# One table of issue times for the end of layer 0's first attention pass, and a longer distance between sums and their products

## The chip, the cores and the metric

The kernel runs on one core of a Trainium2 chip. The metric is the device time of one execution in microseconds (us); the kernel before has a median of 3018.23 us over three runs. PE is TensorE, PEld its weight loads, DVE VectorE, ACT ScalarE, POOL GpSimd, and SP issues the DMAs. L880 is line 880 of the kernel before.

## The reference, cut to what matters

Two layers of a transformer over 1024 image tokens in a 16 x 64 grid and 256 context tokens, width 1024, 16 heads of 64. Layer 0 mixes with neighbourhood attention (a window of 8 x 16 around each query, plus all context tokens), layer 1 with grouped attention over all tokens. Each mixer and each gated feed-forward (hidden width 2816) stands behind a root-mean-square norm with shift, scale and gate that come from a conditioning vector. All is float32 to close accuracy.

```python
def rms_norm(x, g):
    y = xf * lax.rsqrt(jnp.mean(xf * xf, axis=-1, keepdims=True) + EPS)
...
a_l = ada_norm(h, norm_mix[i], sh1_l, sc1_l)
y_l, y_c = neighbourhood_attention_mixer(a_l, a_c, ...)      # layer 0
h = h + g1_l * y_l
h = h + g2_l * swiglu_ffn(ada_norm(h, norm_ffn[i], sh2_l, sc2_l), ffn_w_in[i], ffn_w_out[i])
# the same for the context hc in layer 0
```

## The kernel before, in words

Everything is held transposed: 128 channels on the partitions, tokens along the free axis, in blocks b = 0 and 1 (512 image tokens each) and b = 2 (the 256 context tokens). For accuracy a float32 operand is split into a high and a low part, and a product is three matmuls: high by high, high by low, low by high (`dense_steps`, L770 to L772). The cast to the high part is an ACT instruction, the difference for the low part one of DVE or POOL (L682 and L684 for weights, L812 and L814 for queries and keys, L1868 and L1870 for attention outputs).

Order on each engine is fixed when the program is built. `Lanes` (the object `bg`) keeps a model clock `bg.now` in nanoseconds and a list of background jobs. A job is a Python generator: `pump(credit)` lets the first job issue PE work, where one unit of credit is three matmuls of 512 columns, and `slot(engine)` lets the first waiting piece of side work in lanes 0, 1, 2 issue one instruction on ACT, DVE or POOL. `tick` gives out several slots and one unit, `turn` a third of a unit every 227 ns.

Layer 0's attention is a sequence of *pairs*: two 128-token query tiles of one head. The first pass has three pairs a head, query tiles 0 and 1, tiles 2 and 3, and the two of the context (48 pairs; the context's have only the 256 context keys, and `pump` gets 0.7 more in them). The second pass has two pairs a head (32). A pair's stages are scores (S, X), minima (m, mX, mn), exponentials (e, L849), sums and reciprocals (sr), scaling on POOL (sc, L860), transposes on PE (T, L867), cast and difference (c, s, L875 and L880), products with the values (PV, L497), copy of the output (oc, L889), sum of its parts on POOL (r) and output through a DMA (z). A table, `ORDERA` or `ORDERB`, gives each stage its time relative to the pair's start, with a period from pair to pair (7622 and 5560 ns). `Plan` lays the pairs out by table and sorts all stages by time. In the tables stand filling entries too: PF pumps a given rate of projection work, AF, DF and GF offer a slot of ACT, DVE or POOL. `ORDERA` has three PF, four AF, five DF and three GF a pair, `ORDERB` three PF, two AF, two DF and two GF. The last phase gives its filling for three pairs more.

What fills the pairs: projections of later heads in the order (p, 0), values, (p, 1), then the output projection ("out"), with its weights' splits; DVE products that give the modulation from the conditioning vector (`ada_chunks`, L492, in lane 2, the last); and splits of finished attention outputs (`out_split0`, lane 1). Where a head's projections are not finished when they must be loaded, `until` ticks until they are.

After the plan, what is left of "out" is issued, and layer 0's feed-forward starts with the output projection of block 1 (`project`), which needs the last pair's output. Beside it run three norms: block 0, context, block 1. `norm` squares on ACT (L157), adds the squares up in two running sums (`nacc`, `nacb`) on DVE or POOL (L144), and then `ms_sum` multiplies both with a matrix of ones on PE (L190), which gives the mean to all partitions. Logarithm and exponential on ACT (L177, L179) make the reciprocal root in a tile `nrs`, and `apply` scales the block (L1173; L1305 for the context), shifts it (L1183) and splits it (L955, L952). The three norms share the tiles of the sums and `nrs`. The feed-forward's first products (`mm1`, L1461 to L1463) use a scheme with sums and differences of the blocks: P1 and P2 of five hidden tiles on block 0, with the context beside them, come first, and then P7, which needs differences of both blocks (`sums`) and of the weights.

`ms_sum` waits in the model clock before it issues its products:

```python
while len(added) < count or max(added) + 1200 > bg.now:
    yield ""
```

where `added` holds the model's times at which the running sums are done.

Of the kernel before, what the change touches and what calls it, by code (L numbers as in the profile page):

```python
# [20 lines left out]
KC = D // P  # L21
# [10 lines left out]

V_NMIX, V_NFFN, V_NFIN, V_B, V_QG, V_KG, V_C = 0, 16, 32, 40, 136, 137, 138
V_N = 154
CFG = dict(lag=3, tv=8.0, tm=5.0, t1=43.0, t2=58.0, p0=28, lo="GD", n=39, ra=2.3, rc=0.7, rq=1.1, rb=1.05, gap=263, r1=1.262, lh=300, tk='ADAG', tb=1000000000.0, tg=1, lp='GD')
PERIOD1 = 8172
ORDER1 = {
# [8 lines left out]
PERIODA = 7622  # L46
ORDERA = {
# [6 lines left out]
}  # L54
PERIODB = 5560
ORDERB = {
# [6 lines left out]
}  # L63
# [9 lines left out]
def _build(tc, nc, I, O, top):  # L73
# [62 lines left out]
    def norm(tag, src, there, n, tmp, bank, done, direct=0, line=0):  # L136


        acc, gives, added = [], [], []

        def add(sq, give, engines):
            yield engines
            i = int(bg.engine == "G")
            (v, g)[i].tensor_tensor(acc[i], acc[i], sq, ALU.add)  # L144
            bg.both((690, 1290)[i] * n / 512)
            spent = max(600 + 700 * i, bg.cost)
            added.append(bg.now + spent)
            yield from bg.sleep(spent)
            give()

        ms = None
        for kc in range(KC):
            while not there(kc):
                yield ""
            sq, give = yield from tmp.take("nsq" if kc > 1 else ("nacc", "nacb")[kc], n)
            yield "A0"
            s.activation(sq, src(kc), AF.Square)  # L157
            if kc < 2:
                acc.append(sq)
                gives.append(give)  # L160
            elif kc < KC - direct:
                bg.enter(tag, add(sq, give, "D" if direct or kc >= KC - 2 else "GD"), 800, line)
            else:
                yield from bg.sleep(700)
                if ms is None:
                    ms, free = yield from ms_sum(acc, added, KC - direct - 2, n, bank)
                yield "M"
                t.matmul(ms, lhsT=ones[:], rhs=sq, start=False, stop=kc == KC - 1)
                give()
        if ms is None:  # L170
            ms, free = yield from ms_sum(acc, added, KC - 2, n, bank, True)
        for give in gives:
            give()
        rs, give = yield from tmp.take("nrs", n)
        yield from bg.sleep(2000 if not direct else 1000)
        yield "L"
        s.activation(rs, ms, AF.Ln, bias=eps[:])  # L177
        free()
        s.activation(rs, rs, AF.Exp, scale=-0.5)  # L179
        yield from bg.sleep(1100)  # L180
        yield from done(rs)
        give()

    def ms_sum(acc, added, count, n, bank, stop=False):
        while len(added) < count or max(added) + 1200 > bg.now:
            yield ""
        ms, free = yield from bank()
        yield "M"
        for i in range(2):
            t.matmul(ms[:, :n], lhsT=ones[:], rhs=acc[i], start=i == 0, stop=stop and i == 1)  # L190
        return ms[:, :n], free
# [75 lines left out]
    def startup():  # L267

        ET = mybir.EngineType
        with ExitStack() as ph:  # L270
# [10 lines left out]
            def start(at, gen):  # L281

                heapq.heappush(todo, (at, next(count), gen))
# [9 lines left out]
            def load_raw(k, src):  # L293
                raws[k] = wraw.tile([P, D], F32, name="wr")
                if k[0] == "v":
                    dma(out=raws[k][:].rearrange("p (u n) -> p u n", u=2), in_=src.rearrange("u p n -> p u n"))
                else:
                    dma(out=raws[k][:], in_=src)

            def loads():  # L300
# [12 lines left out]
                for i in range(2):  # L313
                    load_raw(f"v{i}", W[16:18, :, i * 512:i * 512 + 512])
                    start(now + CFG["tv"], split(f"v{i}", w0))
                    yield 1.5
# [15 lines left out]
            def split(k, pool):  # L332
                hi = pool.tile([P, D], F32R, name="wh")
                lo = pool.tile([P, D], F32R, name="wl")
                ws[k] = hi, lo
                s.copy(hi[:], raws[k][:])
                yield 1.2
                v.tensor_tensor(lo[:], raws[k][:], hi[:].bitcast(F32), ALU.subtract)  # L338
# [4 lines left out]
            def c_rows():  # L343
                for w in range(2):
                    for i in range(2):
                        ps = psm.tile([P, 512], F32, name="ps1")
                        dg = tmp.tile([P, 4, P], F32, name="nsq", bufs=2)
                        v.tensor_tensor(dg[:], ident[:].unsqueeze(1).broadcast_to([P, 4, P]),
                                        silc2[:, 4 * i:4 * i + 4, w:w + 1].broadcast_to([P, 4, P]), ALU.mult)
                        t.matmul(ps[:], lhsT=ones[:], rhs=dg[:].rearrange("p a n -> p (a n)"), start=True, stop=True)  # L350
                        yield 0.8
                        s.mul(crow[w][:, i * 512:i * 512 + 512], ps[:], float(D))
                        yield 0.3

            def stat(b):
                n = BLK[b][1]
                acc = []
                for kc in range(KC):
# [10 lines left out]
                    yield 0.55  # L369
                yield CFG["tm"] if b == 1 else 2.0  # L370
                ms = psp.tile([P, 512], F32, name="ms")
# [65 lines left out]
            def first_qk(b):  # L437
# [3 lines left out]
                for kc in range(KC):  # L441
                    while (b, kc) not in ready or b == 0 and min(kc + CFG["lag"], KC - 1) not in ready:
                        yield 0.2
# [20 lines left out]

            for at, gen in [(0.0, loads()), (5.0, c_rows()), (10.0, stat(0)), (CFG["t1"], stat(1)), (CFG["t2"], stat(2)), (28.0, projections())] + \
                    [(max(9.5, a), modulation(m)) for m, a in enumerate((7.0, 13.0, 18.7, 23.0, 26.0, 30.4, 33.3, 36.2))]:
# [32 lines left out]
    class Ring:  # L499
# [4 lines left out]
        def free(self):  # L504
            return self.k < self.n or self.k - self.n in self.back
# [5 lines left out]
        def give(self, k):  # L511
            self.back.add(k)
# [31 lines left out]
    class Lanes:  # L544
# [170 lines left out]
        def tick(self, cost=1.0):  # L715

            self.now += 650
            for e in "TML" + CFG["tk"]:
                if self.busy.get(e, 0) < self.now + CFG["tg" if e == "G" else "tb"]:
                    self.slot(e)  # L720
# [299 lines left out]
    class Ffn:  # L1020
# [97 lines left out]
        def there(self, b, at, k0=0):  # L1118
            return lambda kc: (b, (kc + k0) % KC) in at and at[b, (kc + k0) % KC] <= bg.now

        def src(self, b, k0=0):
            return lambda kc: self.h[b][(kc + k0) % KC]
# [4 lines left out]
        def bank(self):  # L1127
            ps = yield from self.banks.take()
            return ps, lambda: self.banks.give(ps, after=900.0)
# [650 lines left out]
    with ExitStack() as ph:  # L1780
# [6 lines left out]
        bg = Lanes(pb)  # L1787
# [247 lines left out]
        for i, job in enumerate(bg.main[:2]):  # L2035
# [3 lines left out]
        ffn0 = Ffn(0, I["x1"], H0d, lambda m: modB[0][:, m, 0:1], lambda m, b: modB[0][:, 24 + m, which(b):which(b) + 1])  # L2039
        pairs = [[Pair0(h, ps, i) for h in range(HEADS) for i in range(3 - ps)] for ps in range(2)]  # L2040
        n = CFG["n"]
        plan = Plan([(PERIODA, ORDERA, pairs[0][:n], CFG["ra"], 0), (PERIODA, ORDERA, pairs[0][n:], CFG["rq"], CFG["gap"]),
                     (PERIODB, ORDERB, pairs[1], CFG["rb"], 0)])
        load_head(0, 0)
        masks = pb.tile([P, 2, 3, P], F32, name="masks", bufs=1)
        dma(out=masks[:], in_=I["masks"])
# [424 lines left out]
    pairs = [Pair1(h, b) for blk in range(2) for h in range(HEADS) for b in (4 * blk, 4 * blk + 2)]  # L2471
    plan = Plan([(PERIOD1, ORDER1, pairs, CFG["r1"], 0)])
# [173 lines left out]
```

## Time and profile before

| | |
|---|---|
| median of 3 runs | 3018.23 us (3011.64 to 3019.13) |
| the profiled execution | 3023.16 us, span 3021.4 us |
| mean granted TensorE clock | 0.989 |
| PE, DVE, ACT, POOL busy | 97%, 76%, 54%, 41% of the span |
| first pass, pairs 39 to 47 | output copies from 495.8 to 555.5 us |
| second pass, 32 pairs | output copies from 563.8 to 741.4 us |
| layer 0's norms for the feed-forward | products with ones at 769.80, 783.70 and 802.00 us |
| first product P7 | 861.70 us |

The profile shows one execution; its times are counted from the first instruction. "Busy" is the union of an engine's instructions, and matmuls overlap in a pipeline, so a PE that is 97% busy can still be short of its peak. A group line names line, engine, operation, output and inputs, form and count, then busy us and mean ns of one, then the idle time of the engine just before them with what ended it. A line of the timeline begins with start and duration in us, and its bracket holds the idle time before it and what ended that.

### The profile page before, as it was taken

What the parts mean: (1) busy time and instruction counts of PE and PEld (TensorE: products, weight loads), DVE (VectorE), ACT (ScalarE), POOL (GpSimd) and SP (SyncE); (2) the same over time, 40 slices, a digit from 0 to 9 for tenths busy, and PEclk for the clock granted to TensorE, in tenths of its full rate; (3) what the DMA queues carried; (4) which work ended last, traced back from release to release, by engine and by line L of the source; (5) the groups of instructions that cost most, each with busy time, mean ns of one, the idle gap of its engine ahead of it and who ended that gap; (6) DMA issues with size and microseconds to landing.
All of it is one profiled execution on the core that took longest, in us unless ns stands there. A gap on an engine that the chain in (4) does not pass through costs nothing.

```text
span 3021.4 us, 50120 instructions
## 1 busy us (share of the span) xinstructions
PE 2920.2 (97%) x16460; PEld 2506.4 (83%) x16460; DVE 2302.6 (76%) x4659; ACT 1621.6 (54%) x3739; POOL 1247.0 (41%) x1109
## 2 busy tenths in 40 slices
PE   7999999999999999999999899999999999999998
PEld 5888997888788888888888788888888878888886
DVE  7578778876798875557777588899887887776776
ACT  4345545776742322234456489899887632333444
POOL 4246556776244441121121256666643354223112
PEclk8999999999999999999999999999999999999999
DMA  7767767887545562249655523333323333224962
GB/s 265 218 216 238 229 216 232 242 238 214 197 147 192 194 221 80 88 159 323 215 190 196 164 83 94 112 98 102 107 76 124 134 140 121 102 105 150 323 217 108
DMA packets 307170, 519.03 MB, mean 172 GB/s; under 512 B 46432, under 2 KB 112096, under 8 KB 305120
## 3 DMA queue, kind: packets, MB, share of 16 engines
q1 hardware_dynamic: 306912, 515.84, 52.4%
q8 instruction: 131, 2.15, 0.3%
q14 instruction: 127, 1.04, 0.1%
HBM read 389.61 MB, written 120.18 MB: 169 GB/s over the span
## 4 chain that ended last, share of the span: by engine, by line
PE 78%; DVE 10%; DMA 4%; ACT 3%; issue 2%; POOL 2%; SPq 1%; DVEq 0%; ACTq 0%; POOLq 0%
PE pf L1461 9%; PE pf L1462 9%; PE pf L1463 9%; PE T L867 5%; PE o L497 5%; PE pf L1710 5%; PE pf L1709 5%; PE pf L1711 5%; PE ps L770 3%; PE ps L771 3%; PE ps L772 3%; PE S L2254 2%; PE S L2255 2%; DVE pT L880 1%; PE pf L1483 1%
## 5 line engine op out<-in xcount | busy, mean ns | idle before, releaser
L860 POOL TENSOR_SCALAR Pt<-Pt,rc 128x1280 f32<-128x1280 f32 (+3 forms) x288 | 298.8, 1038 | 388.1 <-ACT pT L875 137.6
L880 DVE TENSOR_TENSOR pT<-T,pT 128x256 fp32r<-128x256 f32 (+2 forms) x672 | 341.9, 535 | 35.7 <-ACT pT L875 35.2
L875 ACT CAST pT<-T 128x256 fp32r<-128x256 f32 (+2 forms) x672 | 305.0, 478 | 113.5 <-PE T L867 109.5
L867 PE MATMUL T<-ident,Pt 128*128 128x128 f32 x1952 | 303.0, 275 | 24.3 <-POOL Pt L860 23.2
L867 PEld LDWEIGHTS T<-ident,Pt 128*128 128x128 f32 x1952 | 235.0, 140 | 80.8 <-POOL Pt L860 37.0
L497 PE MATMUL o<-pT,Vt 128*128 128x256 f32 x1952 | 295.2, 290 | 2.3 <-DVE pT L880 2.2
L770 PE MATMUL ps<-ah,wh 128*128 128x512 f32 (+1 forms) x688 | 261.8, 380 | 6.5 <-ACT ah L432 2.6
L497 PEld LDWEIGHTS o<-pT,Vt 128*128 128x128 f32 x1952 | 253.8, 189 | 9.3 <-DVE pT L880 5.7
L771 PE MATMUL ps<-al,wh 128*128 128x512 f32 (+1 forms) x688 | 251.8, 366 | 3.8 <-POOL al L132 2.6
L849 ACT ACTIVATE Pt<-S,rc 128x512 f32<-128x512 f32 (+2 forms) x384 | 247.6, 655 | 9.6 <-DVE rc L841 6.1
L772 PE MATMUL ps<-ah,wl 128*128 128x512 f32 (+1 forms) x688 | 251.2, 365 | 1.4 <-DVE wl L338 1.4
L2246 DVE TENSOR_REDUCE nm<-S 128x1 f32<-128x512 f32 x256 | 169.7, 683 | 35.4 <-PE S L2255 33.7
L952 POOL TENSOR_TENSOR c<-c,c 128x512 f32<-128x512 f32 (+1 forms) x63 | 93.9, 1492 | 246.8 <-DVE c L955 89.6
L955 DVE TENSOR_TENSOR c<-c,c 128x512 fp32r<-128x512 f32 (+1 forms) x166 | 131.9, 809 | 49.3 <-ACT c L1437 34.5
L849 ACT ACTIVATE Pt<-X,rc 128x256 f32<-128x256 f32 x256 | 125.4, 490 | 67.5 <-DVE rc L841 60.8
L1437 ACT CAST wh<-c 128x512 fp32r<-128x512 f32 x112 | 68.8, 618 | 167.2 <-PE pf L1462 62.8
L772 PEld LDWEIGHTS ps<-ah,wl 128*128 128x128 f32 x688 | 131.2, 191 | 23.5 <-DVE wl L338 2.1
L770 PEld LDWEIGHTS ps<-ah,wh 128*128 128x128 f32 x688 | 131.6, 191 | 20.1 <-ACT ah L432 2.8
L1461 PE MATMUL pf<-c,wh 128*128 128x512 f32 x376 | 146.5, 390 | 0.0
L1462 PE MATMUL pf<-c,wh 128*128 128x512 f32 x376 | 146.5, 390 | 0.0
L1463 PE MATMUL pf<-c,wl 128*128 128x512 f32 x376 | 146.3, 389 | 0.0
L895 POOL TENSOR_TENSOR r<-ob 128x256 f32<-128x256 f32 x144 | 123.7, 859 | 54.5 <-ACT ob L889 53.6
(599 smaller groups left out, 9153.4 us busy)
## 6 DMA issues: line engine op xcount, KB each, us to landing
c<-in_fout SPq DMA_DIRECT2D x119, 256.0 KB, 4.0
wr<-in_wqkv SPq DMA_DIRECT2D x53, 512.0 KB, 4.3
wr<-in_adaT SPq DMA_DIRECT2D x96, 256.0 KB, 3.1
c<-in_fin SPq DMA_DIRECT2D x68, 256.0 KB, 3.0
adaw<-in_adaT SPq DMA_DIRECT2D x64, 256.0 KB, 3.8
wr<-in_wo SPq DMA_DIRECT2D x32, 512.0 KB, 4.3
wr<-in_fin SPq DMA_DIRECT2D x58, 256.0 KB, 2.8
K<-Kd SPq DMA_DIRECT2D x64, 224.0 KB, 5.1
```

Source lines behind the costliest of these rows:

```text
L497: t.matmul(o_ap, lhsT=u.V[:, kb, :], rhs=u.pT[:, i, :], start=i == 0, stop=i == len(u.blocks) - 1)
L770: t.matmul(ps, lhsT=hi[:, c], rhs=ah[:, kc, :n], start=kc == 0, stop=False)
L771: t.matmul(ps, lhsT=hi[:, c], rhs=al[:, kc, :n], start=False, stop=False)
L772: t.matmul(ps, lhsT=lo[:, c], rhs=ah[:, kc, :n], start=False, stop=kc == KC - 1)
L849: s.activation(u.Pt[:, off:off + u.wid[c]], u.S[c], AF.Exp, bias=u.min, scale=u.sign, accum_out=u.rc[:, 3 + c:4 + c])
L860: g.tensor_scalar(Pt, Pt, u.rc[:, 2:3], 1.0, ALU.mult, ALU.mult)
L867: t.transpose(T[:, i * P:(i + 1) * P], u.Pt[:, (i0 + i) * P:(i0 + i + 1) * P], ident[:])
L875: s.copy(u.pT[:, i0:i0 + n, :P], u.T[c])
L880: v.tensor_tensor(u.pT[:, i0:i0 + n, P:], u.T[c], u.pT[:, i0:i0 + n, :P].bitcast(F32), ALU.subtract)
L1461: t.matmul(ps[:], lhsT=r32(hi[:, c]), rhs=bh, start=k == 0, stop=False)
L1462: t.matmul(ps[:], lhsT=r32(hi[:, c]), rhs=bl, start=False, stop=False)
L1463: t.matmul(ps[:], lhsT=r32(lo[:, c]), rhs=bh, start=False, stop=k == 3)
```

## The change

The plan had three phases: pairs 0 to 38 by `ORDERA` at rate 2.3, pairs 39 to 47 by `ORDERA` at rate 1.1, and the second pass by `ORDERB` at rate 1.05. It now has two: pairs 0 to 38 as before, then pairs 39 to 47 and the second pass together by `ORDERB` at rate 1.12. The gap of 263 ns stands behind pair 38 in place of pair 47.

`ms_sum` gets its distance as an argument: 3600 ns of the model clock for the three norms of layer 0's feed-forward, and 1200 as before for all others.

```diff
-... rq=1.1, rb=1.05, gap=263, ...
+... rq=1.1, rb=1.12, gap=263, ...
@@ norm
         if ms is None:
-            ms, free = yield from ms_sum(acc, added, KC - 2, n, bank, True)
+
+            ms, free = yield from ms_sum(acc, added, KC - 2, n, bank, True, 3600 if tag == "norm" or tag[:2] == ("norm", 0) else 1200)
@@
-    def ms_sum(acc, added, count, n, bank, stop=False):
-        while len(added) < count or max(added) + 1200 > bg.now:
+    def ms_sum(acc, added, count, n, bank, stop=False, margin=1200):
+        while len(added) < count or max(added) + margin > bg.now:
             yield ""
@@
-        plan = Plan([(PERIODA, ORDERA, pairs[0][:n], CFG["ra"], 0), (PERIODA, ORDERA, pairs[0][n:], CFG["rq"], CFG["gap"]),
-                     (PERIODB, ORDERB, pairs[1], CFG["rb"], 0)])
+
+        plan = Plan([(PERIODA, ORDERA, pairs[0][:n], CFG["ra"], CFG["gap"]),
+                     (PERIODB, ORDERB, pairs[0][n:] + pairs[1], CFG["rb"], 0)])
```

More of the change, by code (lines that the diff above doesn't have):

```diff
@@ L34 @@
 V_N = 154
-CFG = dict(lag=3, tv=8.0, tm=5.0, t1=43.0, t2=58.0, p0=28, lo="GD", n=39, ra=2.3, rc=0.7, rq=1.1, rb=1.05, gap=263, r1=1.262, lh=300, tk='ADAG', tb=1000000000.0, tg=1, lp='GD')
+CFG = dict(lag=3, tv=8.0, tm=5.0, t1=43.0, t2=58.0, p0=28, lo="GD", n=39, ra=2.3, rc=0.7, rq=1.1, rb=1.12, gap=263, r1=1.262, lh=300, tk='ADAG', tb=1000000000.0, tg=1, lp='GD')
 PERIOD1 = 8172
```

## The prediction

> **What bounds the kernel now.** I read the head of the page first, then the busy time by stage, then in each touched stage the waits of PE and the busiest groups of DVE. Columns of a stretch: length; busy us and count of PE, PEld, DVE, ACT, POOL; granted clock; DMA share; GB/s.
>
> ```profile
> span 3021.4 us, 50120 instructions
> PE 2920.2 (97%) x16460; PEld 2506.4 (83%) x16460; DVE 2302.6 (76%) x4659; ACT 1621.6 (54%) x3739; POOL 1247.0 (41%) x1109
> ...
> 372.50:480.90 108.40, 106.48 (x746) 98.82 (x745) 77.77 (x222) 54.39 (x159) 58.27 (x64) 1.00 0.71 221
> 480.90:548.80 67.90, 59.61 (x339) 48.53 (x338) 60.06 (x160) 42.10 (x124) 44.33 (x48) 0.97 0.72 224
> 548.80:580.00 31.20, 29.06 (x191) 25.72 (x190) 26.30 (x89) 25.35 (x78) 21.35 (x25) 1.00 0.84 239
> 580.00:741.00 161.00, 155.38 (x1085) 140.26 (x1084) 126.57 (x440) 123.68 (x377) 120.11 (x141) 1.00 0.83 239
> ```
>
> PE is the bound nearly everywhere, 97% of the span. The exception is 480.9 to 548.8 us, the last nine pairs of the first pass: PE is 88% busy there, DVE also 88%, against 96.5% and 79% in the second pass from 580. So the change works where PE has room. How long a pair takes shows in the copies of its output (count, duration, first and last start), nine for pairs 39 to 47 and 32 for the second pass:
>
> ```profile
> L889 ACT COPY ob<-o x9: 586/586/587, 495.8 to 555.5; 128x512 f32<-128x512 f32 x9
> ...
> L889 ACT COPY ob<-o x32: 586/587/602, 563.8 to 741.4; 128x512 f32<-128x512 f32 x32
> ```
>
> The nine take 563.8 - 495.8 = 68.0 us, 7.55 each; a second-pass pair takes (741.4 - 563.8)/31 = 5.73. The tables say 7.622 and 5.560, so the nine follow their table and the others run behind theirs. What PE waited for in the nine pairs, and what filled DVE and PE there (busy us, mean ns, idle before):
>
> ```profile
> PE T L867 <- POOL Pt L860: 5.4, 6, 1.1
> PE o L497 <- DVE pT L880: 2.2, 6, 0.7
> ...
> L492 DVE CUSTOM_DVE_ANT_0 adaj<-adaw,crow 128x512 f32<-128x512 f32 x16 | 17.6, 1101 | 0.2
> L1870 DVE TENSOR_TENSOR al<-o,ah 128x512 fp32r<-128x512 f32 (+1 forms) x10 | 8.2, 834 | 0.0
> L814 DVE SCALAR_TENSOR_TENSOR ql<-ps,qh 128x512 fp32r<-128x512 f32 (+1 forms) x6 | 3.9, 645 | 0.0
> L684 DVE TENSOR_TENSOR wl<-wr,wh 128x512 fp32r<-128x512 f32 x4 | 3.1, 771 | 0.0
> ...
> L770 PE MATMUL ps<-ah,wh 128*128 128x512 f32 (+1 forms) x46 | 18.5, 402 | 0.0
> ...
> L497 PE MATMUL o<-pT,Vt 128*128 128x256 f32 x69 | 13.4, 303 | 2.3 <-DVE pT L880 2.2
> ```
>
> PE waits for the pair's own chain (scaled rows, transposes, split), because too little lies between its links. Of DVE's 60.06 us, 17.6 + 8.2 + 3.9 + 3.1 = 32.8 us in 36 instructions are filling, more than half of it the modulation products of line 492.
>
> **The change part by part.** *Nine pairs by the second table.* Nothing is computed less; the chain is interleaved more tightly. If the nine ran at 5.73 they would take 51.6 us, 16.4 less: the far end. They hold more projection than a second-pass pair: 46/9 = 5.1 groups of three matmuls each, against
>
> ```profile
> L770 PE MATMUL ps<-ah,wh 128*128 128x512 f32 (+1 forms) x116 | 44.2, 381 | 0.0
> ...
> L497 PE MATMUL o<-pT,Vt 128*128 128x256 f32 x266 | 42.4, 289 | 0.0
> ```
>
> 116/28 = 4.1 (161/5.73 = 28 pairs in the stretch from 580), with wider tiles (402 ns against 381). One group more is about 0.7 us by the 0.68 below. Every third pair (the context's) has less attention: 69/9 = 7.7 products with the values a pair against 266/28 = 9.5, and 1.8 fewer of half a group member's width (0.11) give back 0.2. So 5.73 + 0.5 = 6.2 to 6.3 each, 56.5 in all: a gain of 11.5 us. The near end is that DVE holds them: with all its filling left in, its 60.06 us leave 68.0 - 60.1 = 8 us to win at most, and I put 2 as the least, a quarter of that.
>
> *Slots of DVE.* The first table has five DF slots a pair, the second two: 45 become 18. Of the 36 filling instructions about 24 still fit (18, and some six that the wait for the last projections of head 14 gives out at its ticks), so 12 move into the second pass; line 492 is last in the order of the lanes, so it is these, 12 x 1.1 = 13 us. DVE falls to 47 of 56.5 us in the nine pairs. The second pass has 31.20 - 26.30 = 4.9 us of idle DVE in its first 31 us and 34.4 in the next 161, but takes the 13 in its first eight or nine pairs, about 50 us, with some 10 us idle. Bounds 0 (idle time takes all) and 8 (all inside the first 31 us); I take 2.5, nearer the idle time. The AF slots (four to two) and GF (three to two) carry what they carry in the second pass already. The modulation is needed only after the second pass, so a later end costs nothing of itself.
>
> *Rate 1.12.* 27 slots get 0.02 and 105 (35 x 3, three pairs of filling behind the last) get 0.07 more: 7.9 units. A unit is three 512-column matmuls, and the last of them stand here behind the last output copy:
>
> ```profile
> 741.10 0.39 PE L770 MATMUL ps<-ah,wh 128*128 128x512 f32 x1
> ...
> 741.78 0.39 PE L770 MATMUL ps<-ah,wh 128*128 128x512 f32 x1
> ...
> 748.05 0.40 PE L770 MATMUL pf<-ah,wh 128*128 128x512 f32 x1
> ...
> 754.03 0.49 PE L770 MATMUL pf<-ah,wh 128*128 128x512 f32 x1 [1.03 <-ACT ah L1868]
> ...
> 753.36 0.62 ACT L1868 CAST ah<-o 128x512 fp32r<-128x512 f32 x1 [4.61 <-DMA o<-Od]
> ```
>
> A unit is 741.78 - 741.10 = 0.68 us, so 5.4 us of projection move from behind the last pair into the second pass. In the pass it costs between 0 (all inside PE's idle 3.5% and the small waits) and 5.4; I take 3. Behind the last pair it gains nothing: the block's last output goes through two DMAs and a split (741.4 to 754.03, 12.6 us), and the 6.95 us of projection from 741.10 to 748.05 only cover that. With 1.6 left of it PE waits about 1 + 5.4 us at the same place. Term 0.
>
> *The distance of the sums.* Three norms of layer 0's feed-forward put their two products of ones 2.4 us (3.5 units) later into PE's order.
>
> ```profile
> 769.80 0.67 PE L190 MATMUL pf<-c,ones 128*128 128x512 f32 x1
> ...
> 783.70 0.70 PE L190 MATMUL pf<-c,ones 128*128 128x256 f32 x2 [2.39 <-DVE c L144]
> ...
> 802.00 1.12 PE L190 MATMUL pf<-c,ones 128*128 128x512 f32 x2 [2.85 <-DVE c L144]
> ...
> 803.42 0.79 PE L1461 MATMUL pf<-ah,wh 128*128 128x512 f32 x1
> ...
> 861.70 0.50 PE L1461 MATMUL pf<-ah,wh 128*128 128x512 f32 x1 [1.52 <-ACT wh L1437]
> ```
>
> The context's wait of 2.39 goes: output projections stand ready to move ahead. The 2.85 before the third (block 1) does not: the projections are over, and the first weights of the feed-forward are split only then, so a wait for those takes its place and the products (1.42 us to 803.42) follow later. The first norm (769.80) waits for nothing, so its move is a pure delay of 2.4 us for what hangs on it:
>
> ```profile
> 772.42 0.67 ACT L177 ACTIVATE c<-pf,eps 128x512 f32<-128x512 f32 x1
> ...
> 777.12 0.62 ACT L682 CAST wh<-wr 128x512 fp32r<-128x512 f32 x1 [3.06 <-DMA wr<-in_wo]
> ...
> 797.79 0.72 ACT L1183 ACTIVATE c<-c,modB 128x512 f32<-128x512 f32 x1
> ...
> 799.07 0.47 ACT L177 ACTIVATE c<-pf,eps 128x256 f32<-128x256 f32 x1
> ...
> 810.01 0.49 DVE L134 SCALAR_TENSOR_TENSOR al<-pl,modB,ah 128x256 fp32r<-128x256 f32 x1
> ...
> 814.59 0.69 ACT L177 ACTIVATE c<-pf,eps 128x512 f32<-128x512 f32 x1
> ```
>
> The three share one tile for the root (nrs): the context's logarithm (799.07) follows the last shift of block 0 (797.79), block 1's (814.59) the end of the context's apply (810.01), and from there the sums lead to 861.70, where PE waits. So the first norm's delay reaches PE's next wait, while the 2.39 saved makes PE come earlier to it. If the new place puts the logarithm behind the cast at 777.12, which waited 3.06 us for its DMA, the delay is 5 rather than 2.4. Against it, everything on ACT and DVE that waits for PE's projections moves up by 2.4. Bounds: -3 (2.39 and a little of the 2.85 kept) and +5; I take 0, between a delay and a gain of 2.4 each. PE's 1.52 at 861.70 stays.
>
> *Sum.* -11.5 + 2.5 + 3 + 0 + 0 = -6 us. The profiled execution took 3023.16 us, 4.9 above the median 3018.23 of the runs; so 3017.2 for an execution like it, 3012 for the median.
>
> [...] In the stretches 500 to 505 and 505 to 510 the granted clock was low although PE's longest wait among the pairs is 1.1 us:
>
> ```profile
> 500.00:505.00 5.00, 3.32 (x14) 2.40 (x13) 4.34 (x11) 4.09 (x14) 4.55 (x6) 0.81 0.79 253
> 505.00:510.00 5.00, 5.00 (x29) 4.40 (x28) 4.90 (x14) 2.50 (x10) 2.71 (x4) 0.85 0.61 191
> 740.00:755.00 15.00, 13.74 (x75) 11.50 (x74) 3.41 (x8) 2.87 (x5) 6.34 (x7) 1.00 0.55 158
> ```
>
> That loss was 5 x 0.19 + 5 x 0.15 = 1.7 us. [...]
>
> **The rivals.** *All of the room is won (28%).* The nine pairs run at the second pass' 5.73 (-16.4), the 13 us of DVE and the 5.4 of PE vanish half in idle time (+2), the context's 2.39 is kept (-2): about -14, that is 3004. For it: DVE is idle 34.4 us of the second pass, and its visible PE waits are short. Against: the nine carry more projection.
>
> *The nine pairs are held by DVE, and the table matters little (12%).* The least of 2 us is won, and with 3 for the rate the time is 3019. For it: DVE is busy 4.90 of 5 us from 505. Against: the filling that makes it so loses its slots.
>
> *The norms' chain costs more than the pairs win (12%).* Block 0's logarithm falls behind the cast that waits for its DMA: 5 us, and as the two running sums are shared as well, the context's norm adds its own 2.4, block 1's another: up to 9.8 at 861.70. From a delay of 6 on the kernel is slower than before; with the full one the time is 3018 - 6 + 9.8 = 3022. For it: the shared tile shows in the order 797.79, 799.07, 810.01, 814.59. Against: PE's own place moves up.
>
> *The clock falls behind the last pair (10%).* The rate takes 5.4 us of cover from a wait of 1.03, and if the clock then falls as it did at 500, the same 1.7 us is lost: -4.3, that is 3014. For it: the two rows from 500. Against: 1.00 in the row from 740. [...]
>
> **How the numbers follow.** A measurement here tells about 0.3%, 9 us, from no change. My forecast 3012 (38%) covers 3008 to 3016 by itself; the rivals 28, 12, 12 and 10%. Faster by over 0.3% (below 3009): the first rival, and a little of the forecast: 0.31. Slower by over 0.3% (above 3027): only the far part of the chain's case and what I have not seen: 0.09. Within: 0.60. The range 3001 to 3022 reaches from -17 (the first rival's ends all taken) to the chain's case.
>
> **What would show it.** The nine output copies 6.2 to 6.3 us apart; line 492 running into the second pass, by some eight pairs; second-pass pairs at about 5.8 to 5.9; after the last copy 12 to 13 us to the split of the last block, with a PE wait of 5 to 7 us; no PE wait at the context's products of ones, a new one ahead of the first feed-forward matmul, and the wait at the difference weights (861.70 before) about as long as now. I am wrong if the nine pairs stay above 7 us, if the second pass grows by over 6 us, or if the feed-forward's first wait grows by more than 4.

## The result and the profile after

The changed kernel takes 3024.23 us in the median of 8 runs, against 3017.08 for the kernel before in 8: a ratio of 1.0023, 95% interval 1.0013 to 1.0034. That is 7 us slower, small but outside the scatter; a second comparison, below, gives 1.0020 (1.0010 to 1.0030). The forecast was 3012, with 3001 to 3022 as its range.

The two profiled executions hide this: 3024.11 us after and 3023.16 before, because the one before lies 6 us above its median (3.5 us of that are lost before pair 30, where both kernels are the same: its output copy starts at 411.4 in the trace before, at 407.8 in the one after). So I compare stages within the traces and take totals from the runs.

The head of the page after, the output copies of pairs 39 to 48 and of the second pass, and the busy time by stage (columns as before). Lines from 170 on are one higher than before, from about 2040 on two:

```profile
span 3022.1 us, 50109 instructions
PE 2917.2 (97%) x16460; PEld 2504.8 (83%) x16460; DVE 2297.4 (76%) x4663; ACT 1621.4 (54%) x3739; POOL 1244.8 (41%) x1105
...
L890 ACT COPY ob<-o x10: 586/589/597, 494.8 to 546.8; 128x512 f32<-128x512 f32 x10
...
L890 ACT COPY ob<-o x32: 586/587/599, 546.8 to 735.0; 128x512 f32<-128x512 f32 x32
...
494.80:546.80 52.00, 51.38 (x313) 44.13 (x313) 43.26 (x134) 41.97 (x122) 38.77 (x43) 1.00 0.84 254
546.80:570.00 23.20, 21.43 (x140) 18.43 (x139) 20.56 (x72) 20.12 (x61) 19.03 (x21) 1.00 0.93 256
570.00:625.00 55.00, 41.09 (x276) 34.08 (x275) 45.78 (x162) 41.44 (x130) 43.12 (x48) 1.00 0.86 240
625.00:735.00 110.00, 105.53 (x731) 96.09 (x730) 83.75 (x287) 78.44 (x238) 77.62 (x89) 0.98 0.77 227
```

The nine pairs won more than forecast: 546.8 - 494.8 = 52.0 us against 68.0, and PE is busy 99% there. Not all of the 16 us is kept, because the copies of pairs 30 to 39 come 2.5 us further apart than before: from the copy of pair 30 to that of pair 48 it is 139.0 us against 152.4, 13.4 less. Then the second pass takes 735.0 - 546.8 = 188.2 us against 177.6. (That 177.6 is long for its table: in the four other kernels with the old tables the second pass takes 174.5 to 176.9 in the trace.) The hole stands in one row: from 570 to 625 PE is busy 41 of 55 us, 75%, and no other compute engine is busy for more than 84% of it. The first matmul of each group of three (high by high, line 770 before, 771 after) and the waits of PE in that stretch tell which work is missing. Before, the same pairs (586 to 644) held 39 such matmuls; after, 11:

```profile
586.00:644.00 58.00, 15.16 (x39) 7.42 (x40) 1.00 0.88 252
```

```profile
570.00:625.00 55.00, 4.09 (x11) 2.08 (x11) 1.00 0.86 240
...
PE X L2000 <- ACT Pt L850: 6.2, 7, 1.1
PE T L868 <- POOL Pt L861: 5.8, 7, 1.5
PE S L1983 <- DMA K<-Kd: 1.0, 1, 1.0
PE T L868 <- DVE rc L842: 0.8, 2, 0.4
```

PE waits for links of the pair's own chain, as it did in the nine pairs before the change, because there is no projection to lay between them. The output projection needs the split attention outputs of block 0 and of the context. These are 16 DVE instructions, 8 of 512 and 8 of 256 columns. Before, the last of the 16 starts at 595; after, 10 have started by 580 and the 16 (among 18) only by 622:

```profile
L1870 DVE TENSOR_TENSOR al<-o,ah x16: 415/684/1342, 494.7 to 595.0; 128x512 fp32r<-128x512 f32 x8, 128x256 fp32r<-128x256 f32 x8
```

```profile
L1871 DVE TENSOR_TENSOR al<-o,ah x10: 415/726/1071, 491.7 to 579.4; 128x512 fp32r<-128x512 f32 x8, 128x256 fp32r<-128x256 f32 x2
...
L1871 DVE TENSOR_TENSOR al<-o,ah x18: 415/682/1071, 491.7 to 621.7; 128x512 fp32r<-128x512 f32 x10, 128x256 fp32r<-128x256 f32 x8
```

What DVE did in the nine pairs in their place (groups of DVE, after):

```profile
L685 DVE TENSOR_TENSOR wl<-wr,wh 128x512 fp32r<-128x512 f32 x8 | 6.7, 839 | 0.0
...
L1871 DVE TENSOR_TENSOR al<-o,ah 128x512 fp32r<-128x512 f32 x4 | 3.2, 810 | 0.0
```

Weights' splits went from 4 to 8 on DVE, outputs' splits from 10 to 4, and the modulation products of line 492 are no longer among the large groups; the last one starts at 657.5 us, against 534.4 before. The projection that wasn't issued is made up behind the last pair: from the last output copy to the first projection of the feed-forward it is now 15.0 us (735.0 to 750.05) against 6.7 (741.4 to 748.05).

The norms' part, in the timeline of PE, and the granted clock around it:

```profile
786.37 0.91 PE L191 MATMUL pf<-c,ones 128*128 128x256 f32 x3 [0.36 <-DVE c L144]
...
803.41 0.80 PE L1462 MATMUL pf<-ah,wh 128*128 128x512 f32 x1 [5.18 <-ACT wh L1438]
...
865.28 0.50 PE L1462 MATMUL pf<-ah,wh 128*128 128x512 f32 x1 [1.40 <-ACT wh L1438]
...
800.00:803.40 3.40, 0.00 (x0) 0.00 (x0) 3.21 (x6) 3.16 (x8) 1.27 (x1) 0.71 0.32 116
803.40:806.00 2.60, 2.59 (x6) 1.84 (x7) 2.60 (x5) 1.93 (x4) 0.00 (x0) 0.50 0.70 223
806.00:808.00 2.00, 2.00 (x7) 1.54 (x6) 2.00 (x6) 0.51 (x1) 0.00 (x0) 0.50 0.88 280
```

Of the context's wait 0.36 us is left, a wait of 5.18 us stands ahead of the first feed-forward product, and behind it the clock is at half. Before, the same stretch ran at full clock behind a wait of 2.85:

```profile
803.40:806.00 2.60, 2.60 (x12) 1.98 (x11) 2.60 (x6) 1.52 (x4) 0.00 (x0) 1.00 0.80 276
```

Twelve matmuls in 2.6 us against six. From the first feed-forward product to the first difference product it is 61.9 us after (803.41 to 865.28) and 58.3 before (803.42 to 861.70). The wait at the difference product itself is as long as before (1.40 and 1.52).

### The profile page after: what moved, and what is told of

The parts are those of the page before. It is cut to its first block, busy times and chain, and to the rows that moved or that the text cites. A ratio compares the mean times of both kernels' runs of the same rounds, so it can differ in the third digit from the quotient of the medians.

```text
span 3022.1 us, 50109 instructions
## 1 busy us (share of the span) xinstructions
PE 2917.2 (97%) x16460; PEld 2504.8 (83%) x16460; DVE 2297.4 (76%) x4663; ACT 1621.4 (54%) x3739; POOL 1244.8 (41%) x1105
## 4 chain that ended last, share of the span: by engine, by line
PE 78%; DVE 9%; ACT 4%; DMA 3%; POOL 3%; issue 2%; SPq 1%; DVEq 0%; POOLq 0%; ACTq 0%
PE pf L1462 9%; PE pf L1464 9%; PE pf L1463 9%; PE T L868 5%; PE o L498 5%; PE pf L1710 5%; PE pf L1711 5%; PE pf L1712 5%; PE ps L771 3%; PE ps L772 3%; PE ps L773 3%; PE S L2256 2%; PE S L2257 2%; POOL Pt L861 1%; PE pf L1485 1%
```

## The experiments

All are compared with the kernel before on the same chip, five rounds each. "Slots" in the names means slots in pairs 39 to 47.

**Which half of the change loses.** Tables and rate alone, then distances alone:

```diff
 # tables_only, on the changed kernel
-... 3600 if tag == "norm" or tag[:2] == ("norm", 0) else 1200)
+... 1200)
 # margins_only, on the kernel before: the two edits of norm and ms_sum alone
```

> The changed kernel with the distance of the sums put back to 1200 ns for all norms, so only the tables and the rate differ from before. If the norms' part costs what the two traces suggest (PE waits 5.18 us ahead of the first feed-forward product, then runs at a clock of 0.50 to 0.71 for about 5 us, against 2.85 + 2.39 us of waits before), this kernel is 3 to 6 us faster than the changed one: 3018 to 3021, within 4 us of before. The wait ahead of the context's products comes back (about 2.4 us), the one ahead of the first feed-forward product is under 1 us, the clock stays at 1.00 there. Rival: the norms are neutral and all of the loss is in the second pass; then it is 3024 like the changed kernel.

> The kernel before with only the longer distance of the three sums. If the norms' part loses, it is 3 to 6 us slower than before (3020 to 3023), with no wait at the context's products, 4 to 6 us of wait ahead of the first feed-forward product and a clock well below 1.00 for some us behind it. Rival, as the prediction had it: 0, the 2.39 us saved pay for the rest.

Tables alone: 1.0007 (0.9998 to 1.0016). Distances alone: 1.0009 (0.9998 to 1.0019). Neither is clear of zero by itself. Of the signs expected for the tables one did not come: the clock did not stay at 1.00 (0.61 from 806 to 810 us in that trace). Those for the distances came: 5.2 us of wait ahead of the first feed-forward product, a clock of 0.52 over the 4 us behind it, and 0.27 us at the context's products. Both together were 1.0023, so I ran the changed kernel and the tables side by side:

> The changed kernel itself, beside the tables alone on the same chip. If the distances of the sums are part of its loss, it is 2 to 5 us slower than the tables alone; if all of the loss is the tables', the two agree within 1.5 us. By the stages of the traces the distances should come to about zero here (projections 3.3 us shorter, the stages to the first difference product 3.2 us longer).

> The tables and the rate alone, distance 1200 throughout: about +0.1 to +0.2% to before.

Changed kernel 1.0020 (1.0010 to 1.0030), tables alone 1.0005 (0.9995 to 1.0015): medians of 3024.74 and 3018.53 us. So here the distances carry the larger part of the loss: 0.15%, 4.5 us, or 6.2 us by the medians, where the two traces had suggested about zero. The intervals just overlap, and the distances alone came to 0.09%, so the size stays rough. The tables win nothing: what the nine pairs gain is given back.

**Why the tables win nothing.** In pairs 39 to 47, the table gets slots back. In the model's order of issue, each split of an attention output takes one ACT slot, then one DVE slot, then loads the next.

```diff
+        more = dict(ORDERB, DF2=1600, DF3=4600, AF2=1300)   # slots_da; slots_d without AF2, slots_a with AF2 alone
         plan = Plan([(PERIODA, ORDERA, pairs[0][:n], CFG["ra"], CFG["gap"]),
-                     (PERIODB, ORDERB, pairs[0][n:] + pairs[1], CFG["rb"], 0)])
+                     (PERIODB, more, pairs[0][n:], CFG["rb"], 0), (PERIODB, ORDERB, pairs[1], CFG["rb"], 0)])
```

> The changed kernel, and in pairs 39 to 47 the second table gets two more slots for DVE (at 1600 and 4600) and one more for ACT (at 1300). Theory 1, the splits of the attention outputs ran short of slots (each needs one of ACT and one of DVE in turn), so that the output projection had nothing to issue from 565 to 622 us: the second table's nine pairs still take about 52 us, projection runs on through 565 to 622, the last output copy moves 3 to 8 us forward (727 to 732 against 735), and the first projection of the feed-forward 5 to 8 us (742 to 745 against 750); time 5 to 8 us below the changed kernel, 3016 to 3019. Theory 2, DVE's displaced work (13 us) made DVE the bound in the second pass: two more DVE slots a pair keep that work in the nine pairs, which take 56 us or more, and the sum stays at 3022 to 3026.

> As slots_da, but only the two slots of DVE are added, none of ACT. Theory 1 in its strict form (the splits alternate between ACT and DVE, so that DVE slots alone are taken by the modulation products): the modulation is finished within the nine pairs, but the projection still stands still from about 565 to 622 us, and the time stays that of the changed kernel, 3022 to 3026. If DVE's slots were what was missing (theory 2, or my prediction's reading that DVE's slots are the scarce ones), it gains as much as slots_da: 3016 to 3019.

> The changed kernel with only the one ACT slot more in pairs 39 to 47, none of DVE. Each split takes an ACT slot and then a DVE slot. In the order of issue the second split group ends between the changed kernel's and the one with both, and the output projection is done 3 to 4 us of the model's clock earlier than in the changed kernel: about a third of the way, 3020 to 3023 (+0.05 to +0.15%). If ACT's slots alone were the cause, it equals the kernel with both (-0.12%).

Both engines' slots: 0.9988 (0.9979 to 0.9997). DVE's alone: 1.0029 (1.0019 to 1.0039). ACT's alone: 1.0009 (0.9999 to 1.0019). The first matmuls of a group from 570 to 625 go with it, 36 with both, 8 with DVE's, 21 with ACT's:

```profile
570.00:625.00 55.00, 13.39 (x36) 6.79 (x36) 1.00 0.77 226
...
L1871 DVE TENSOR_TENSOR al<-o,ah x16: 411/680/1159, 492.7 to 596.3; 128x512 fp32r<-128x512 f32 x8, 128x256 fp32r<-128x256 f32 x8
```

```profile
570.00:625.00 55.00, 3.32 (x8) 1.50 (x8) 0.97 0.81 228
```

```profile
570.00:625.00 55.00, 7.72 (x21) 3.98 (x21) 0.97 0.75 216
```

(slots_da, slots_d, slots_a in this order.) With both, the last of the 16 splits starts at 596, as it did before the change; with DVE's slots alone at 627, with ACT's alone at 613. So the projection starved because its splits ran short of slots, and both engines were short, ACT the more: its slot alone brings back part of the projection, while more DVE slots alone only let the modulation products run earlier (the last at 522 in place of 657). The rival, that displaced DVE work bounds the second pass, is out: slots_d keeps that work in the nine pairs and is the slowest of all, even beyond the 3022 to 3026 expected (3028).

Two details of slots_da were not as expected. Its nine pairs take 56.2 us, not 52, and the last output copy stays where it was (734.7 against 735.0). What is won lies behind it: 2.6 us to the feed-forward's first projection in place of 15.0.

**What the distances cost, one by one,** each on the kernel before:

```diff
+ ... True, 3600 if tag == ("norm", 0, 1) else 1200)    # margin_b1; margin_b0: ("norm", 0, 0); margin_ctx: "norm"
```

> The kernel before with the longer distance for block 1's norm alone. The wait of 2.85 us moves from the products of ones to the first feed-forward product and grows to 4 to 5 us, the granted clock falls to 0.5 to 0.7 for about 5 us behind it, and the stage from there to the first difference product grows from 58.3 to about 61.5: +2 to +4 us. Rival: the distance of block 0's norm, through the shared tile, is what costs; then this kernel equals the one before.

> The kernel before with the longer distance for the context's norm alone. The wait of 2.39 us at the context's products goes, nothing else changes: the projections take about 49 in place of 51.1 us, the stages behind keep their length; -1 to -2.5 us. Rival (the prediction's): what is saved is waited for again at the first difference product, which hangs on the chain of the norms: that wait grows from 1.5 to 4 us, and the time is unchanged.

> The kernel before with the longer distance for block 0's norm alone. My prediction made this the one that delays the chain of the norms (by 2.4 us, or 5 behind a cast that waits for its DMA), so that the wait at the first difference product grows from 1.5 us: +2 to +5 us. If that chain has slack (the later norms start when they did), it is within 1.5 us of before and the wait there stays 1.5.

Block 1's: 1.0009 (1.0000 to 1.0017). The context's: 1.0007 (0.9999 to 1.0016). Block 0's: 1.0000 (0.9991 to 1.0009). The waits of PE in the feed-forward's start, margin_b1, margin_ctx, margin_b0:

```profile
PE pf L1461 <- ACT wh L1437: 4.8, 2, 3.3
PE pf L190 <- DVE c L144: 2.1, 1, 2.1
```

```profile
PE pf L190 <- DVE c L144: 5.1, 1, 5.1
PE pf L1461 <- ACT wh L1437: 1.5, 1, 1.5
```

```profile
PE pf L190 <- DVE c L144: 5.5, 2, 3.3
PE pf L1461 <- ACT wh L1437: 1.4, 1, 1.4
```

Each is inside the scatter or at its edge, so the traces tell more here than the totals. Block 1's distance does what was expected: the wait moves to the first product (3.3 of the 4.8 us, where 4 to 5 was expected), and the stage behind it is 61.4 us. The 2.1 us left at line 190 is the context's. The context's distance is a miss. I expected -1 to -2.5 us: the context's wait is gone, but block 1's grows from 2.85 to 5.1, because PE comes to it 2 us earlier and its sum, on a DVE that is busy 16.27 of 19 us there, is not ready earlier; and then the clock falls as well, to 0.50:

```profile
790.00:794.30 4.30, 0.04 (x1) 0.04 (x1) 3.81 (x8) 3.58 (x9) 0.00 (x0) 0.66 0.47 164
794.30:797.00 2.70, 2.70 (x4) 1.15 (x5) 2.70 (x6) 2.47 (x5) 0.00 (x0) 0.50 0.66 225
...
sum 19.00, PE 13.30 PEld 9.44 DVE 16.27 ACT 13.05 POOL 1.35; mean PE 2.66 PEld 1.89 DVE 3.25 ACT 2.61 POOL 0.27
```

Block 0's distance costs nothing that can be measured, and the wait at the first difference product stays 1.4: the chain through the shared tile has the slack for it. In its trace the context's wait grew to 3.29 us and the clock was 0.62 over the 4 us behind it, and still the ratio is 1.0000.

**The rate, and the best version.** On the repaired tables I tried the distance for the context alone with both rates, then 1200 throughout, with one more ACT slot, with both rates:

```diff
 # slots_da_ctx: slots_da with 3600 for the context's norm alone;  slots_da_ctx_r105: the same, rb=1.05
 # t_da: slots_da with 1200 for all;  t_daa: t_da with AF3=3400 besides;  t_daa_r105: the same, rb=1.05
```

> The kernel with the added slots (two of DVE, one of ACT in pairs 39 to 47), and the longer distance kept for the context's norm alone; the two 512-column norms go back to 1200 ns. If the distance of block 1's norm is what costs (a wait of 4 to 5 us ahead of the first feed-forward product and a lowered clock behind it), the stage from the first feed-forward product to the first difference product falls from 61.7 to about 58.5 us, the context's wait stays away, and the time is 2 to 4 us below the kernel with the added slots: 3013 to 3015 beside a before of 3018. Rival: the distance is neutral, and it stays at -0.12%.

> As the one before, with the rate back at 1.05. If the rate only moves projection from behind the last pair, where it covers the way of the last output, into the second pass, where PE has little room, the second pass gets some 3 us shorter (183.2 to about 180), the wait ahead of the last output's use gets shorter by as much as the cover grows (3.7 us to near 0), and the time is 2 to 4 us less than at 1.12. Rival: the rate fills idle time in the second pass, then 1.05 is slower by up to 3 us or the same.

> The tables' part alone (distance 1200 for all norms) with two DVE slots and one ACT slot more in pairs 39 to 47. Beside the kernel with the same slots and the long distances (-0.12%, 3.6 us under before) it tells what the distances cost when the projection doesn't starve: if they cost, the stage from the last projection to the first difference product is 62 to 63 us in place of 65.8 and the projections stand some 2 us longer, 1 to 2 us less in all; -0.15 to -0.2% to before. If they are neutral: -0.12%.

> As t_da, with a second ACT slot more (at 3400) in pairs 39 to 47. In the order of issue both attention-output splits are then done by the time the projection wants them, so PE should have projection without a break in the second pass' first pairs: the waits of PE between 565 and 625 us fall below 3 us (about 10 in t_da's sister), the second pass takes 178 to 181 us in place of 183, and the time is -0.2 to -0.3% to before. Rival: with the break gone, the pairs become longer by the projection issued in them, and nothing is won over t_da.

> As t_daa with the rate at 1.05. Without the starved stretch this is the clean test of the rate. If the denser rate only moves covering work from behind the last pair (the prediction's term of +3), this is 0 to 3 us faster than t_daa; if the rate fills idle time, it is 2 to 6 us slower, as the earlier pair of kernels (1.12 at -0.13%, 1.05 at +0.14%) suggests.

In order: 0.9987 (0.9979 to 0.9996), 1.0014 (1.0005 to 1.0023), 0.9986 (0.9975 to 0.9998), 0.9995 (0.9985 to 1.0006), 1.0002 (0.9992 to 1.0011). So no loss by the higher rate shows: 1.12 is ahead in both pairs. In the second, the clean one, it is inside the scatter (3 us). In the first it is ahead by 8 us, but this is no price of the rate in itself: at 1.05 the splits are late again (the last of the context's at 621 against 596, with 17 first matmuls from 570 to 625 against 36), and 11.0 us stand between the last copy and the feed-forward against 2.6. Why they are late there is not shown.

Three of these kernels beat the one before and can't be told apart: slots_da, slots_da_ctx and t_da, whose median is the lowest (3011.67 us beside 3018.13). In the stages from its last projection to the first difference product t_da takes 4.2 + 58.3 us, against 4.1 + 61.7 in slots_da, which has the longer distances; but the totals, 0.9986 and 0.9988, don't differ. So with the projection repaired the distances cost nothing that shows, which was the rival that slots_da_ctx was to tell apart. The second added slot of ACT was a miss: the splits are done earlier (the last of the context's starts at 572 in place of 596), but PE gets no more projection from 570 to 625 (36 in both), the nine pairs get longer (58.1 us against 56.3) and nothing is won.

## Why the prediction was wrong

*Nine pairs by the second table: the mechanism right, the size low.* -11.5 was forecast, 56.5 us for the nine; they took 52.0, -16.0, nearly the far end, of which 13.4 is left when counted from pair 30. DVE fell to 43.3 us there, where 47 was forecast, so it did not hold them.

*Slots: here the prediction failed.* It named DVE's slots, counted 12 instructions that would move, and took all of them for the modulation products, which nobody waits for soon. Two readings were wrong. First, that the last in order gives way alone: weights' splits took twice as many DVE slots as before, and six of the ten outputs' splits gave way too. Second, the sentence that ACT's two slots "carry what they carry in the second pass already": in these nine pairs they have to carry the outputs' splits beside the weights', and slots_a and slots_d show both engines short. In place of the +2.5 for DVE's load stood the price of a job that had nothing to issue: +10.6 us in the second pass and +8.3 behind the last pair. The projections behind that took 2.9 us less, but some 2 of these are the context's wait, which belongs to the distances. The prediction had named a second pass grown by over 6 us as a sign of being wrong, and it came.

*The rate: no loss to be seen.* +3 was forecast; at 1.12 neither comparison is slower than at 1.05, and the clean one (t_daa) is 3 us faster, inside the scatter. The reading that PE in the second pass had little room for it is not borne out. The reading of the tail held in direction where the projection isn't starved: in slots_da the last output's use waits 3.69 us, against 1.03 before (5 to 7 was forecast). In the changed kernel it does not wait at all, since the late projection covers it. Behind that wait in slots_da the clock fell too, to 0.50 from 746 to 750:

```profile
746.00:750.00 4.00, 4.00 (x9) 2.88 (x10) 1.53 (x4) 1.65 (x3) 1.29 (x1) 0.50 0.95 320
```

*The distances: the waits right, the price of 0 wrong in this kernel.* The context's wait went and a new one came ahead of the first product, as forecast, though with 5.18 us it is over the 4 us that the prediction had named as a sign of being wrong; the term was 0 with +5 as its bound, and the side by side runs give 4.5 to 6 us. The reason for the upper bound, the chain through block 0 and the shared tile, costs nothing by itself (margin_b0). What the prediction left out there is the clock, which was 0.50 behind the wait of 5.18; whether that is the price stays open (last section).

*The rivals.* The first was right on the nine pairs and wrong that the rest vanishes in idle time. The second (DVE holds the nine) and the third (the norms' chain) are refuted. The clock's case did not come out as it stood: behind the changed kernel's last pair PE has no wait (busy 15.00 of 15.00 us from 735 to 750) and the clock is 1.00. It fell elsewhere, to 0.50 each time: in the last pair at 729.7, at the feed-forward's first product and at the first difference product. In the tail and the norms it was 0.62 over the 4 us behind a wait of 3.29 (margin_b0), 0.50 over the 4 us behind one of 3.69 (slots_da) and 0.50 behind those of 5.1 (margin_ctx) and 5.18 (the changed kernel). It stayed at 1.00 behind 2.85 in the kernel before, and fell to 0.50 behind 1.40 at the changed kernel's difference product.

## What to carry to other kernels

When an order of issue is thinned out, count the slots by engine for each job that other work waits for, not only the load of the busiest engine: here a job that alternates between two engines had both slots short, and what it held back starved an engine that was not short of anything (36 first matmuls from 570 to 625 with slots of both added, 21 with ACT's, 8 with DVE's, 11 with none). A wait removed on an engine that is ahead of its neighbours can come back at the next meeting point, so ask what the engine meets next: in margin_ctx the context's 2.39 us went and block 1's 2.85 grew to 5.1. And add PE's waits up over a few microseconds, not only the longest: at 503.1 us in the kernel before, the clock fell to 0.50 after 3.42 us in which PE was busy for 1.74 and no wait was over 1.1.

## What the hardware showed that I had not expected

After 5.18 us without work the granted clock was 0.50 for the next 4.6 us, in which 13 matmuls ran against 29 in the same stretch before (806 to 808 held 7 against 17). But the falls don't go by the length of one wait: the clock fell at a wait of 1.40 us and stayed at 1.00 behind one of 2.85. In the two traces, of the kernel before and of the changed one, the clock has only the values 1.00 and 0.50, and within a trace its changes lie whole multiples of 3.41 us apart. Take the periods of that length from 300 to 1000 us that ran at full clock, in both traces together. In two PE was busy for 7% and 28%, and the next period ran at half clock. In eight it was busy for 43 to 61%, and the next ran at half clock twice, after 51% (before) and 52% (after), but not after 43% and another 51% (both before). In the other 393, with 63% or more, the next never did. Three periods, each with the one behind it: at the changed kernel's wait of 5.18, at its difference product with a wait of only 1.40, and at the wait of 2.85 in the kernel before:

```profile
798.00:801.41 3.41, 0.23 (x1) 0.00 (x0) 3.10 (x4) 3.38 (x7) 1.39 (x2) 1.00 0.52 185
801.41:804.83 3.42, 1.42 (x3) 0.95 (x4) 3.42 (x7) 3.21 (x8) 0.62 (x1) 0.50 0.61 210
...
862.85:866.26 3.41, 1.76 (x11) 1.12 (x9) 3.41 (x6) 2.55 (x5) 1.18 (x1) 1.00 0.17 59
866.26:869.68 3.42, 3.24 (x8) 2.56 (x9) 3.42 (x6) 1.31 (x3) 1.27 (x1) 0.50 0.16 56
```

```profile
800.07:803.48 3.41, 1.48 (x5) 0.77 (x5) 3.41 (x8) 2.89 (x7) 0.00 (x0) 1.00 0.51 170
803.48:806.89 3.41, 3.41 (x17) 2.68 (x16) 3.41 (x8) 1.65 (x5) 0.00 (x0) 1.00 0.81 258
```

The fall at 503.1 us in the kernel before, which the prediction has in its rows from 500, is of the same kind: PE was busy 1.74 of the 3.42 us ahead of it, with no single wait over 1.1, and the next 3.41 us ran at 0.50. The two periods of 51% show that the busy share of one period does not settle it. The mean granted clock differs between executions of one and the same kernel: in the 12 of the tables alone (tables_again) it is 0.988 in the longest, of 3027.98 us, and 0.995 in the shortest, of 3013.18.

In the changed kernel's trace PE worked 4.83 us at half clock behind the wait of 5.18 (1.42 and 3.41 in two periods), which, with half of that time counted as lost, is an estimated 2.4 us of the 3.6 by which that stage is longer, and 3.24 us behind the difference product, an estimated 1.6. Over many executions the clock is not shown to be the distances' price. The mean granted clock is 0.9905 over the 12 executions of the changed kernel and 0.9915 for the tables alone beside it, but 0.9914 both for the distances alone and for the kernel before beside them. How much of the price is the clock, and how much the products that now stand among the feed-forward's, stays open.
